# Hybrid decoder trunk on one core: keys' low parts packed once instead of twice, and one weight cast placed behind the value evictions

## Chip, core and metric

The kernel runs on one core of a Trainium2 chip. The metric is the device time of one execution in microseconds (us); lower is better. One matrix engine (PE), a vector engine (DVE), a scalar engine (ACT), a general engine (POOL) and a queue engine (SP) work side by side; SP and POOL issue the DMAs that matter here.

## What is computed

Two layers over 512 tokens of width 1024 in float32. Each layer normalises x, multiplies it by a joint input matrix that feeds three head groups (a short gated convolution, differential attention with rotary, a Conformer convolution of 31 taps), adds the joint output projection to x, and then adds a SwiGLU block. The attention is the part around the change:

```python
q = apply_rope(q.reshape(b, s, 2, N_DIFF_HEADS, DIFF_HEAD_DIM), cos, sin)
k = apply_rope(k.reshape(b, s, 2, N_DIFF_HEADS, DIFF_HEAD_DIM), cos, sin)
v = v.reshape(b, s, N_DIFF_HEADS, DIFF_V_DIM)
...
sc = jnp.einsum("bqmhd,bkmhd->bmhqk", qi, k) * scale
p = jax.nn.softmax(jnp.where(mask, sc, -jnp.inf), axis=-1)
a = p[:, 0] - lam * p[:, 1]
return jnp.einsum("bhqk,bkhe->bqhe", a, v)
```

There are four heads of two maps (m = 0, 1) with 64 channels each and 128-dim values.

## The kernel before

**Products in three passes.** Every float32 operand of a large product is split into a high part, rounded to the format fp32r in which PE multiplies, and a low part, the rest. A product is then three matmuls, high by high, high by low and low by high (`mm3`, lines 182 to 188).

**The weight pipeline.** All weights lie in one list of units of 512 KB in the order of use. `load` (line 110) brings a unit into one of three raw buffers, through POOL's queue for units 5 to 32 of a layer and through SP's for the rest. A unit is two halves, and each half is one tile `w` of [128, 2, 512] out of six. `prep` (line 124) fills it: ACT casts raw to the high part (line 135); then either DVE subtracts it from raw (lines 144 and 154), or, for most halves of the attention's stretch, ACT writes minus raw (line 137) and a DMA of POOL adds the weights to it from memory (line 138). That is, such a half costs ACT two instructions and POOL one DMA `w<-wu`. `next_half` (line 152) hands out the next half and calls `prep` for the ones ahead, up to five. While the list `held` is not empty, the furthest half is written down there instead of being prepared, and `release` (line 171) prepares what was written down later. Each engine executes in the order in which the program is written, so the place of `prep` in the code sets the place of its casts on ACT.

**Queries and keys.** `qk_units` computes the even and odd halves of the rotary pairs of two heads on PE, `turn_qk` (line 408) rotates them on DVE into tiles `ro`, and `split_and_pack` (line 425) splits them into `hl` (high and low) and moves the pieces to where the scores want them, with 16 DMAs of SP per call. For the queries, `pq` holds for each map the high part in partitions 0 to 63 and the low part in 64 to 127. For the keys, `pk` has four planes of [128, 512]: plane 2m holds the high part in both halves of the partitions, plane 2m+1 the low part in both halves. One DMA for each of the 16 pieces moves 32 partitions of 2 x 512 values (128 KB). There are two `pk` tiles (two heads of a pair) and two buffers, so that both pairs of both layers use the same two buffers. The scores (`Pair.scores`, lines 489 to 491) are, for each map, one matmul of `pq` with plane 2m, one with plane 2m+1, and one that adds the causal mask.

**Values.** `values` (line 453) multiplies h by the values' weights, with eight halves of weights and four PSUM results. ACT evicts the four results into `vt` (line 467). The results lie in both buffers of the PSUM pool `sc`, and the scores need a buffer of that pool: the first scores wait for the first two evictions.

**Slots.** After the values the program goes slot by slot (`slot`, line 774): PE does the scores of block b, six wide matmuls of filler work (`fill(2)`, two weight blocks), the attention values of block b-2, the transposes `pT` of block b-1, and six more wide matmuls. Between them DVE finds the maxima `nm` of the scores (line 493), does one tap of the 31-tap convolution (line 578) and combines the two maps into `e` (line 507), and ACT does the exponentials (line 497). The transposes of block b-1 wait for `e` of that block. During the values, `each` puts three taps behind each of the eight weight halves on DVE. The filler is the second pair's queries and keys first, then the short convolution.

Of the kernel before, what the change touches and what calls it, by code (L numbers as in the profile page):

```python
# [19 lines left out]
F32 = mybir.dt.float32  # L20
F32R = mybir.dt.float32r
# [7 lines left out]
S = 512  # L29
L = 2  # L30
P = 128
# [4 lines left out]
HD = 64  # L36
# [42 lines left out]
def trunk(ctx, tc, xT, pos, wu, cv, lamv, cst, out):  # L79
    nc = tc.nc  # L80
    V, A, G, T = nc.vector, nc.scalar, nc.gpsimd, nc.tensor

    def pool(name, bufs, **kw):
        return ctx.enter_context(tc.tile_pool(name=name, bufs=bufs, **kw))
    cp = pool("cp", 1)
# [4 lines left out]
    pk = pool("pk", 2)  # L90
# [32 lines left out]
    def prep(i, ahead=True):  # L123


        if i >= 2 * L * UNITS or i in wtiles:
            return
        u, half = divmod(i, 2)
        load(u)
        for k in range(1, 2 + half if ahead else 1):  # L130
            load(u + k)
        raw = wraw[u][:, half, :]
        t = pw.tile([P, 2, 4 * P], F32R, tag="w", name=f"w{i}")
        wtiles[i] = t
        A.copy(t[:, 0, :], raw)  # L135
        if 4 <= u % UNITS < 30 and (i % 3 == 1 or u % UNITS >= 12):
            A.mul(t[:, 1, :], raw, -1.0)  # L137
            G.dma_start(t[:, 1, :], wu[u, :, 4 * P * half:4 * P * half + 4 * P], accum_op=ALU.add)  # L138
        else:
            sub = functools.partial(V.tensor_sub, t[:, 1, :], raw, t[:, 0, :].bitcast(F32))  # L140
            if ordered[0] and i > 5:
                subs.append(sub)
            else:
                sub()  # L144
# [17 lines left out]
    held = []  # L162

    def release():

        for i in held[1:]:
            prep(i)
        del held[:]
# [21 lines left out]
    def side_by_side(n):  # L190


        for k in range(KC - n):
            w = next_half()
            for j in range(4):
                yield k, j, w
        ws = [next_half() for _ in range(n)]
        for j in range(4):
            for k in range(n):
                yield KC - n + k, j, ws[k]  # L200

    def four(name):
        ps = [sc.tile([P, 2, S], F32, tag="sc", name=f"{name}{i}") for i in range(2)]
        return [ps[i // 2][:, i % 2, :] for i in range(4)]
# [11 lines left out]
    def start():  # L216


        nc.sync.dma_start(cvt, cv)
        nc.sync.dma_start(x[0], xT[0])  # L220
        load(0)
        nc.sync.dma_start(x[1], xT[1])
        load(1)
        nc.sync.dma_start(x[2], xT[2])
        nc.sync.dma_start(x[3], xT[3])
        load(2)
        nc.sync.dma_start(x[4], xT[4])
        ones_d = cp.tile([P, P], F32, name="ones_d")
        pi = pt.tile([P, P], I32, tag="t", name="posi")
        G.dma_start(pi, pos)  # L230
        lv = pt.tile([P, L, 4, HD], F32, tag="t", name="lv")
        G.dma_start(lv, lamv.partition_broadcast(P))
        G.dma_start(ones_d, cst[:, 1, :])
        cs = pt.tile([P, 2, P], F32, tag="t", name="cs")
        G.dma_start(cs, cst[:, 0::2, :])
        warm = sm.tile([P, 1], F32, tag="nm", name="warm")
        V.memset(warm, 0.0)
        A.activation(warm, warm, AF.Sin)

        wz = pt.tile([P, S], mybir.dt.bfloat16, tag="t", name="wz")  # L240
        V.memset(wz, 0.0)
        wp = tp.tile([P, S], F32, tag="tp", name="wp")
        for _ in range(10):
            T.matmul(wp, lhsT=wz[:, :P], rhs=wz, start=True, stop=True)
        ones_r = cp.tile([P, P], F32R, name="ones_r")
        idr = cp.tile([P, P], F32R, name="idr")
        maskr = cp.tile([P, P], F32R, name="maskr")
        G.tensor_copy(ones_r, ones_d)
        G.tensor_copy(idr, cs[:, 0, :])
        G.tensor_copy(maskr, cs[:, 1, :])  # L250
        consts.update(ones_d=ones_d, ones_r=ones_r, idr=idr, maskr=maskr, ident=idr.bitcast(F32), pi=pi, lv=lv)
# [133 lines left out]
            yield  # L385

    pending = []
    gates = []

    def later():  # L390

        while pending:
            pending.pop(0)()
# [15 lines left out]
    def turn_qk(isk, ps, cosr, sinr, packs):  # L409

        t = [pt.tile([P, S], F32, tag="t", name=f"ro{i}") for i in range(4)]
        V.tensor_mul(t[0], ps[0], cosr)
        V.tensor_mul(t[1], ps[0], sinr)
        yield
        V.tensor_mul(t[2], ps[1], sinr)
        V.tensor_mul(t[3], ps[1], cosr)
        V.tensor_sub(t[0], t[0], t[2])
        V.tensor_add(t[1], t[1], t[3])
        if not packs:
            packs += [[pk.tile([P, n, S], F32R, tag=tag, name="p" + tag) for tag, n in (("q", 2), ("k", 4))]  # L420
                      for _ in range(2)]
        pending.append(functools.partial(split_and_pack, isk, t, packs))
        yield

    def split_and_pack(isk, t, packs):
        hls = [pr.tile([P, 2, S], F32R, tag="hl", name="hl") for _ in range(2)]
        for ab in range(2):
            if isk:
                A.copy(hls[ab][:, 0, :], t[ab])
            else:  # L430
                A.mul(hls[ab][:, 0, :], t[ab], QS)
        for ab in range(2):
            o, hl = t[ab], hls[ab]
            if isk:
                V.tensor_sub(hl[:, 1, :], o, hl[:, 0, :].bitcast(F32))
            else:
                V.scalar_tensor_tensor(hl[:, 1, :], o, QS, hl[:, 0, :].bitcast(F32), ALU.mult, ALU.subtract)
        for hh in range(2):
            q, k = packs[hh]
            for ab in range(2):  # L440
                hl = hls[ab]
                for m in range(2):
                    src = slice(64 * hh + 32 * m, 64 * hh + 32 * m + 32)
                    for d in range(2):
                        dst = slice(64 * d + 32 * ab, 64 * d + 32 * ab + 32)
                        eng = nc.sync
                        if isk:
                            eng.dma_start(k[dst, 2 * m:2 * m + 2, :].bitcast(F32), hl[src].bitcast(F32))
                        else:
                            eng.dma_start(q[dst, m, :].bitcast(F32), hl[src, d, :].bitcast(F32))  # L450

    def values(h, rT, each):
        ws = four("v")
        for n, (k, b, w) in enumerate(side_by_side(1)):
            t = slice(b * P, b * P + P)
            T.matmul(ws[b], lhsT=h[k][:, 0, t], rhs=w[:, 0, :], start=k == 0, stop=False)
            T.matmul(ws[b], lhsT=h[k][:, 0, t], rhs=w[:, 1, :], start=False, stop=False)
            T.matmul(ws[b], lhsT=h[k][:, 1, t], rhs=w[:, 0, :], start=False, stop=k == KC - 1)
            if n == 3:
                later()  # L460
            if n % 4 == 3:
                each(n // 4)
        vt = []
        for b in range(4):
            if b % 2 == 0:
                t = pv.tile([P, 2, S], F32, tag="v", name=f"vt{b}")
            A.activation(t[:, b % 2, :], ws[b], AF.Copy, scale=rT[:, b:b + 1])
            vt.append(t[:, b % 2, :])
        return vt

    class Pair:
# [170 lines left out]
    def mixing(l, h, run, each):  # L642
# [3 lines left out]
        packs = [[], []]  # L646


        pq = [acc.tile([P, S], F32, tag="acc", name="qk") for _ in range(2)] if l == 0 else []
# [8 lines left out]
        if l == 0:  # L658
            start()

            hs = []

            def chunk(k):
                h.append(make_h(k, C_MIXG))
                if k:
                    hs.append(add_square(k - 1, hs[-1] if hs else None, V, True))
            rt = rope_tables()
            next(rt)
            prep(0, False)
            chunk(0)  # L670
            prep(1, False)
            chunk(1)
            next(rt)
            lam = lambdas()
            for k in range(6):
                lead[0] = (1, 2, 2, 3, 3, 3)[k]
                chunks([k])
                if k < 3:
                    nc.sync.dma_start(x[k + 5], xT[k + 5])
                chunk(k + 2)  # L680
                if k == 0:
                    state["tab"] = next(rt)
                if k == 1:
                    next(lam)
            hs.append(add_square(KC - 1, hs[-1], V, True))
            run = hs[-1]
            lead[0] = AHEAD - 1
        else:
            chunks(range(6))
# [237 lines left out]
    for l in range(L):  # L927
# [24 lines left out]
        for half in range(2):  # L952
            acts = []
            for f in range(FH):
# [8 lines left out]
                t = pt.tile([P, S], F32, tag="t", name="tg")  # L963
# [128 lines left out]
```

## Time and profile before

| what | value |
| --- | --- |
| median of 3 runs | 1172.51 us (1172.22 to 1177.48) |
| the profiled execution's own time | 1169.26 us |
| its span in the profile | 1167.4 us |
| PE busy | 1137.1 us, 97% of the span |
| DVE, ACT, POOL busy | 637.2, 502.6, 198.5 us |
| mean granted TensorE clock | 0.986 of full |
| DMA traffic | 141.68 MB in 50342 packets |

The terms of the prediction are read from one execution, the profiled one; the runs without a profile lie 3.25 us higher in the median. PE has work for nearly the whole span, so time is won or lost where PE waits, or where it works at the lower of its two clock levels.

### The profile page before, as it was taken

Reading aid. Unit: us, or ns where it says so; the run is one execution under the profiler, and the core shown is the slowest. Engines: PE = TensorE matmul, PEld = TensorE weight load, DVE = VectorE, ACT = ScalarE, POOL = GpSimd, SP = SyncE. Lnnn points to the kernel's source line nnn. Section 1 sums busy time; section 2 is a strip of 40 time slices with the busy share of each in tenths; the row PEclk is TensorE's granted clock in tenths of the full one; section 3 lists DMA queues with packets and bytes.
Section 4 is the critical chain, followed back from the end, with each engine's and each line's share of the span. In section 5 each row is a group of like instructions: output and inputs, shape, how many; then the busy total and the mean of one; then the engine's idle time right before and its main releaser. Section 6 shows DMA issues by size and latency. Waiting matters only on the chain.

```text
span 1167.4 us, 14339 instructions
## 1 busy us (share of the span) xinstructions
PE 1137.1 (97%) x5238; PEld 943.8 (81%) x5238; DVE 637.2 (55%) x1140; ACT 502.6 (43%) x1034; POOL 198.5 (17%) x229
## 2 busy tenths in 40 slices
PE   8989899999999999999999899999999999999995
PEld 6878787788888888888888788877888888888885
DVE  6777786654443344444448788657444333444445
ACT  6546566643332233333334467765333222333323
POOL 2222223311100011010112222332111000011001
PEclk9989899999999999999999899999999999999998
DMA  7785847432332322322337878663223223223212
GB/s 228 190 211 130 197 109 165 106 126 91 104 95 90 109 91 94 105 90 99 102 98 177 195 170 190 139 158 97 102 90 106 93 91 108 91 94 105 90 55 73
DMA packets 50342, 141.68 MB, mean 121 GB/s; under 512 B 7104, under 2 KB 9408, under 8 KB 50272
## 3 DMA queue, kind: packets, MB, share of 16 engines
q1 hardware_dynamic: 29888, 88.79, 23.7%
q0 software_dynamic: 20384, 51.98, 19.5%
q8 instruction: 41, 0.67, 0.2%
q14 instruction: 29, 0.24, 0.1%
HBM read 125.93 MB, written 2.23 MB: 110 GB/s over the span
## 4 chain that ended last, share of the span: by engine, by line
PE 85%; DMA 4%; DVE 4%; issue 3%; ACT 2%; SPq 1%; POOL 1%; DVEq 0%; ACTq 0%; POOLq 0%
PE od L186 8%; PE od L188 8%; PE od L187 8%; PE gp L188 7%; PE gp L187 7%; PE up L187 7%; PE up L188 7%; PE up L186 7%; PE gp L186 6%; PE qk L186 3%; DMA raw<-wu 2%; PE qk L187 2%; PE qk L188 2%; PE cc L186 1%; PE cc L187 1%
## 5 line engine op out<-in xcount | busy, mean ns | idle before, releaser
L135 ACT CAST w<-raw 128x512 fp32r<-128x512 f32 x384 | 237.6, 622 | 495.1 <-PE od L188 146.0
L144 DVE TENSOR_TENSOR w<-raw,w 128x512 fp32r<-128x512 f32 x265 | 187.1, 707 | 239.8 <-ACT w L135 239.2
L966 POOL TENSOR_TENSOR tg<-tg,r 128x512 f32<-128x512 f32 x44 | 57.8, 1316 | 520.3 <-ACT tg L965 510.7
L187 PE MATMUL gp<-h,w 128*128 128x512 f32 x352 | 137.2, 390 | 0.6 <-DVE h L263 0.6
L186 PE MATMUL up<-h,w 128*128 128x512 f32 x352 | 137.2, 390 | 0.1
L188 PE MATMUL gp<-h,w 128*128 128x512 f32 x352 | 137.1, 390 | 0.0
L186 PE MATMUL gp<-h,w 128*128 128x512 f32 x352 | 137.1, 390 | 0.0
L187 PE MATMUL up<-h,w 128*128 128x512 f32 x352 | 137.0, 389 | 0.0
L188 PE MATMUL up<-h,w 128*128 128x512 f32 x352 | 137.0, 389 | 0.0
L186 PE MATMUL od<-act,w 128*128 128x512 f32 x328 | 127.6, 389 | 0.0
L187 PE MATMUL od<-act,w 128*128 128x512 f32 x328 | 127.6, 389 | 0.0
L188 PE MATMUL od<-act,w 128*128 128x512 f32 x328 | 127.6, 389 | 0.0
L138 POOL DMA_DIRECT2D w<-wu x82 | 72.7, 887 | 240.0 <-ACT w L137 217.9
L578 DVE SCALAR_TENSOR_TENSOR acc<-pad,cvt,acc 128x511 f32<-128x511 f32 (+14 forms) x120 | 88.0, 734 | 2.8
L187 PEld LDWEIGHTS gp<-h,w 128*128 128x128 f32 x352 | 66.1, 188 | 15.1 <-DVE h L263 1.5
L186 PEld LDWEIGHTS up<-h,w 128*128 128x128 f32 x352 | 66.1, 188 | 14.6 <-DVE x L932 1.0
L186 PEld LDWEIGHTS gp<-h,w 128*128 128x128 f32 x352 | 66.1, 188 | 14.1 <-ACT h L262 0.5
L188 PEld LDWEIGHTS up<-h,w 128*128 128x128 f32 x352 | 66.1, 188 | 13.8
L188 PEld LDWEIGHTS gp<-h,w 128*128 128x128 f32 x352 | 66.1, 188 | 13.6
L187 PEld LDWEIGHTS up<-h,w 128*128 128x128 f32 x352 | 66.1, 188 | 13.6
L188 PEld LDWEIGHTS od<-act,w 128*128 128x128 f32 x328 | 61.6, 188 | 12.9
L187 PEld LDWEIGHTS od<-act,w 128*128 128x128 f32 x328 | 61.6, 188 | 12.7
(255 smaller groups left out, 1982.0 us busy)
## 6 DMA issues: line engine op xcount, KB each, us to landing
raw<-wu SPq DMA_DIRECT2D x135, 512.0 KB, 3.5
raw<-wu POOLq DMA_DIRECT2D x56, 512.0 KB, 6.0
w<-wu POOLq DMA_DIRECT2D x82, 256.0 KB, 4.8
pk<-hl SPq DMA_DIRECT2D x64, 128.0 KB, 6.3
pq<-hl SPq DMA_DIRECT2D x64, 64.0 KB, 3.7
x<-xT SPq DMA_DIRECT2D x8, 256.0 KB, 7.5
yT<-fo SPq DMA_DIRECT2D x8, 256.0 KB, 2.5
raw<-wu SPq DMA_DIRECT2D x2, 256.0 KB, 4.9
```

Source lines behind the costliest of these rows:

```text
L135: A.copy(t[:, 0, :], raw)
L138: G.dma_start(t[:, 1, :], wu[u, :, 4 * P * half:4 * P * half + 4 * P], accum_op=ALU.add)
L144: sub()
L186: T.matmul(ps, lhsT=hi, rhs=rh[:, 0, :], start=first, stop=False)
L187: T.matmul(ps, lhsT=hi, rhs=rh[:, 1, :], start=False, stop=False)
L188: T.matmul(ps, lhsT=lo, rhs=rh[:, 0, :], start=False, stop=last)
L578: V.scalar_tensor_tensor(a[:, d:], pad[:, :S - d], cvt[:, c - d:c - d + 1], a[:, d:], ALU.mult, ALU.add)
L966: G.tensor_mul(t, t, r)
```

## The change

Three things. The keys' tiles become two permanent tiles `pk0` and `pk1`; the lower 64 partitions of planes 1 and 3 are set to zero once, by four memsets on POOL in layer 0. The DMAs of the keys leave these places out: of the 16 of a call, eight move 32 x 1024 values as before and eight move 32 x 512. So the second matmul of the scores multiplies the queries' high part with the keys' low part, and leaves out low by low, which stood in it before. Third, `values` puts a mark into `held` after the sixth of the eight halves, and calls `release` behind the evictions: the furthest halves that the last two halves of the values ask for are noted, and only what is still noted at the end is prepared behind the evictions.

```diff
+    keys = [cp.tile([P, 4, S], F32R, name=f"pk{hh}") for hh in range(2)]
+
+    def zero_rows():
+        for t in keys:
+            for m in range(2):
+                G.memset(t[HD:, 2 * m + 1, :].bitcast(F32), 0.0)
...
         if not packs:
-            packs += [[pk.tile([P, n, S], F32R, tag=tag, name="p" + tag) for tag, n in (("q", 2), ("k", 4))]
-                      for _ in range(2)]
+            packs += [[pk.tile([P, 2, S], F32R, tag="q", name="pq"), keys[hh]] for hh in range(2)]
...
-                        if isk:
+                        if isk and d == 0:
                             eng.dma_start(k[dst, 2 * m:2 * m + 2, :].bitcast(F32), hl[src].bitcast(F32))
+                        elif isk:
+                            eng.dma_start(k[dst, 2 * m, :].bitcast(F32), hl[src, 0, :].bitcast(F32))
...
             if n % 4 == 3:
                 each(n // 4)
+            if n == 23:
+                held.append(None)
         vt = []
         for b in range(4):
             if b % 2 == 0:
                 t = pv.tile([P, 2, S], F32, tag="v", name=f"vt{b}")
             A.activation(t[:, b % 2, :], ws[b], AF.Copy, scale=rT[:, b:b + 1])
             vt.append(t[:, b % 2, :])
+        release()
         return vt
...
             run = hs[-1]
+            zero_rows()
             lead[0] = AHEAD - 1
```

On ACT, around the evictions of layer 0 (w is a weight half, raw its unit, vt a value result), before:

```order
L135 CAST w_763<-raw_703 128x512
L137 ACTIVATE w_763<-raw_703 128x512
L135 CAST w_784<-raw_703 128x512
L137 ACTIVATE w_784<-raw_703 128x512
L135 CAST w_803<-raw_742 128x512
L137 ACTIVATE w_803<-raw_742 128x512
L467 ACTIVATE vt_822<-v_638,rT 128x512 x2
L467 ACTIVATE vt_825<-v_639,rT 128x512 x2
L497 ACTIVATE e,lsum<-ps,nm 128x128 x2
```

and with the change:

```order
L135 CAST w_767<-raw_707 128x512
L137 ACTIVATE w_767<-raw_707 128x512
L135 CAST w_803<-raw_707 128x512
L137 ACTIVATE w_803<-raw_707 128x512
L477 ACTIVATE vt_822<-v_642,rT 128x512 x2
L477 ACTIVATE vt_825<-v_643,rT 128x512 x2
L135 CAST w_828<-raw_746 128x512
L137 ACTIVATE w_828<-raw_746 128x512
L508 ACTIVATE e,lsum<-ps,nm 128x128 x2
```

One half's pair of instructions, the first of the unit raw_742 (raw_746 in the change), has moved behind the four evictions and stays ahead of the first exponentials; in layer 1 the same pair moves. The orders of PE and DVE are the same in both programs.

On POOL, at the place of the memsets in layer 0 (cosr is the cosine table, fetched from memory):

```order
L118 DMA raw_328<-wu 128x1024
L138 DMA w_345<-wu 128x512
L118 DMA raw_367<-wu 128x1024
L394 MEMSET pk_109 64x512 x2
L394 MEMSET pk_110 64x512 x2
L709 DMA cosr<-tab_dram 32x512 x4
L118 DMA raw_445<-wu 128x1024
```

The four memsets stand ahead of the four cosine DMAs and of the weight loads that follow; nothing else on POOL has moved.

## Rows read from the trace of the kernel before

**Rows 1.** Waits of PE over the span: us in total, times, longest.
```profile
PE ps L489 <- ACT vt L467: 7.3, 2, 4.2
PE ps L489 <- DMA pk<-hl: 5.6, 2, 4.4
...
PE ssps L301 <- DVE fo L897: 1.6, 1, 1.6
```

**Rows 2.** Timeline of ACT, layer 0: start us, us, instruction, [idle before <-releaser].
```profile
74.56 0.63 ACT L137 ACTIVATE w<-raw 128x512 fp32r<-128x512 f32 x1
77.73 0.62 ACT L135 CAST w<-raw 128x512 fp32r<-128x512 f32 x1 [2.54 <-DMA raw<-wu]
...
78.78 2.41 ACT L467 ACTIVATE vt<-v,rT 128x512 f32<-128x512 f32 x4
```

**Rows 3.** Timeline of PE, layer 0.
```profile
80.08 0.48 PE L489 MATMUL ps<-pk,pq 128*128 128x128 f32 x1 [4.21 <-ACT vt L467]
...
86.63 0.28 PE L489 MATMUL ps<-pk,pq 128*128 128x256 f32 x1
...
88.72 0.27 PE L516 MATMUL pT<-idr,e 128*128 128x128 f32 x1
```

**Rows 4.** Timeline of PE, layer 1.
```profile
653.62 0.47 PE L489 MATMUL ps<-pk,pq 128*128 128x128 f32 x1 [3.14 <-ACT vt L467]
...
662.19 0.27 PE L516 MATMUL pT<-idr,e 128*128 128x128 f32 x1
```

**Rows 5.** Stretches: busy us of each engine (count), PEclk, DMA share, GB/s.
```profile
79.80:86.50 6.70, 6.42 (x18) 5.35 (x19) 3.48 (x8) 3.23 (x9) 1.65 (x3) 0.50 0.93 232
134.40:141.10 6.70, 5.85 (x15) 4.66 (x16) 3.92 (x8) 2.46 (x7) 0.85 (x1) 0.50 1.01 241
...
653.20:659.90 6.70, 6.28 (x18) 5.22 (x19) 3.74 (x8) 3.37 (x9) 1.79 (x3) 0.50 1.05 265
...
1152.00:1156.00 4.00, 2.42 (x18) 1.94 (x17) 1.93 (x5) 1.90 (x5) 2.14 (x4) 1.00 0.03 11
```

**Rows 6.** Timeline of DVE, both layers.
```profile
69.97 11.53 DVE L578 SCALAR_TENSOR_TENSOR acc<-pad,cvt,acc 128x503 f32<-128x503 f32 x15
81.67 0.42 DVE L493 TENSOR_REDUCE nm<-ps 128x2 f32<-128x256 f32 x1 [0.17 <-PE ps L491]
...
83.47 0.35 DVE L507 SCALAR_TENSOR_TENSOR e<-e,c 128x128 f32<-128x128 f32 x1
...
643.72 11.45 DVE L578 SCALAR_TENSOR_TENSOR acc<-pad,cvt,acc 128x498 f32<-128x498 f32 x15
...
657.01 0.35 DVE L507 SCALAR_TENSOR_TENSOR e<-e,c 128x128 f32<-128x128 f32 x1
```

**Rows 7.** Chain that ended last: start us, us, what (a wide filler matmul; keys of pair 1).
```profile
107.80 0.23 PE qk L187
...
130.67 4.57 DMA pk<-hl
...
700.01 5.14 DMA pk<-hl
```

**Rows 8.** Timeline of ACT, layer 1.
```profile
648.32 0.62 ACT L137 ACTIVATE w<-raw 128x512 fp32r<-128x512 f32 x1
```

**Rows 9.** The stretch in which pair 1's keys are packed, columns as in rows 5.
```profile
126.00:131.00 5.00, 4.83 (x25) 3.90 (x23) 4.12 (x9) 4.24 (x12) 1.01 (x3) 1.00 1.03 227
```

**Rows 10.** POOL's two-input operation, of the page's costliest groups: busy us, mean ns.
```profile
L966 POOL TENSOR_TENSOR tg<-tg,r 128x512 f32<-128x512 f32 x44 | 57.8, 1316 | 520.3 <-ACT tg L965 510.7
```

**Rows 11.** DMA issues: out<-in, engine, op xcount, KB each, median us to landing.
```profile
pk<-hl SPq DMA_DIRECT2D x64, 128.0 KB, 6.3
...
cosr<-tab_dram POOLq DMA_DIRECT2D x8, 64.0 KB, 4.9
```

**Rows 12.** Timelines of POOL and of DVE around the cosine table, layer 0.
```profile
28.45 2.24 POOL L697 DMA_DIRECT2D cosr<-tab_dram  x4
...
40.81 0.69 DVE L703 TENSOR_TENSOR cosr<-cosr,r 128x512 f32<-128x512 f32 x1 [1.35 <-ACT r L340]
```

**Rows 13.** Landing of the DMA w<-wu that POOL issues at 67.1 us.
```profile
DMA to landing us min/median/max: 12.4/12.4/12.4
```

## Prediction

> **What bounds the kernel now.** The page first: PE is busy for 97% of the span, so only its waits and its clock can be won back. The list of PE's waits [rows 1] names two causes of weight: the first scores wait for the value evictions (7.3 us, once in each layer), and scores wait for the packed keys (5.6 us in two waits, 4.4 and 1.2). Then the timeline of ACT [rows 2] says why the evictions are late: the cast at 77.73 stands ahead of them, and ACT sat idle 2.54 us before it, for a weight transfer that had not landed. The evictions start only at 78.78, and PE, free since 80.08 - 4.21 = 75.87 [rows 3], starts the scores 1.30 us after that. In layer 1 PE waits 3.14 us at the same place [rows 4].
>
> The stretches [rows 5] show what each of these waits costs beside its own length: behind the value wait of layer 0, behind the long key wait and behind the value wait of layer 1 the granted clock is 0.50, the lower level of 1.2 GHz, for at least 6.7 us, in which full speed would have done the same work in half the time. Two waits of the profile are too short for that: the clock is 1.00 around the wait of 1.6 us near the end [rows 1, 5].
>
> Last the timeline of DVE [rows 6], because it is next in line: it does fifteen taps without a pause from 69.97 to 81.50 and reaches the first maxima `nm` at 81.67, having waited only 0.17 us for PE. The combined `e`, on which PE's first transposes hang, ends at 83.47 + 0.35 = 83.82. In layer 1 the taps end at 643.72 + 11.45 = 655.17 and `e` at 657.36.
>
> **The change, part by part.**
>
> *The cast behind the evictions, layer 0.* ACT's instruction ahead of the late cast starts at 74.56 [rows 2]; its neighbours follow one another 0.53 us apart, so ACT is free for the evictions at 75.09, not at 78.78. With the same 1.30 us to PE, the scores start at 76.39 instead of 80.08, a wait of 0.5 us, and no fall of the clock. That would save 3.7 us of wait and half of PE's 6.42 busy us at the low clock [rows 5], 6.9 us. But PE doesn't get that far. From the second scores to the first transposes it needs 88.72 - 86.63 = 2.09 us at full clock [rows 3]; of these 6 x 0.23 = 1.4 are six wide matmuls [rows 7], so that the first slot (scores and twelve wide ones) takes 3.5. PE stands before the transposes at 76.39 + 3.5 + 2.09 = 82.0, and `e` is there at 83.82 less DVE's 0.17 of waiting, 83.65, since DVE's taps are not moved. So PE waits a new 1.7 us, and with 0.1 for the handover passes the transposes at some 83.75 instead of 88.72: **4.97 us** won. Were the evictions earlier still, this would be the same.
>
> *Layer 1.* ACT is free at 648.32 + 0.53 = 648.85 [rows 8], before PE ends the values at 653.62 - 3.14 = 650.48 [rows 4], so nothing is left of the first wait. PE stands before the transposes at 650.5 + 3.5 + 2.09 = 656.1, `e` ends at 657.36, a new wait of 1.3 us; passed at 657.46 instead of 662.19: **4.73 us**.
>
> *What the moved cast delays.* Its transfer lands just before 77.73, when the four evictions (2.41 us from 75.09) are through at 77.5. So the cast stays where it was in time, and so does POOL's DMA behind it; the exponentials queued behind it on ACT wait for `nm` until after 81.9 anyway. Cost 0.
>
> *Fewer bytes of keys.* Of each 16 key DMAs eight shrink from 128 to 64 KB; their number on SP stays. For the first head of pair 1 (eight DMAs, four smaller) that is 4 x 64 KB = 0.26 MB. The DMA engines are full while they move (share 1.03, 227 GB/s [rows 9]), so the last of the eight lands 0.26 MB / 227 GB/s = 1.15 us earlier than 130.67 + 4.57 = 135.24 [rows 7]. I take 1.1. Below, nothing is gained if the landing is all latency. Above, 2.2 us, if the other queue's transfers that share the engines are held up in proportion and give back as much again. In layer 0 the key wait of 4.4 falls to 3.3 us: **1.1 us**, and the clock still falls, as it did behind the 3.14 us of layer 1 [rows 4, 5]. In layer 1 the keys land at 700.01 + 5.14 = 705.15, and 1.1 of the 1.2 us wait goes: **1.1 us**. The other pairs' keys are not waited for. By the page "DMA: Bandwidth & Descriptors" of the Trainium skill, section "Queues, rings and completion order", a DMA engine takes turns between queues by whole packets; smaller packets of one queue then give back their own time and not the other queue's, which would keep the sum as it is, while sharing by bytes would bring it to 1159.4. No row here shows the turns.
>
> *The memsets.* Four on POOL, each between nothing and POOL's two-input operation of that width, 1.32 us [rows 10]; at most 5.3 us together. I take the upper end. Behind them stand the cosine DMAs, issued by 28.45 + 2.24 = 30.69, landing 4.9 us later at the median [rows 11, 12], 35.6; DVE reads the table at 40.81, and waited there for ACT, not for it. That is 5.2 us of cover: cost 0. With that cover gone, a lateness of DVE at 40.81 would pass on to the queries.
>
> *Permanent key tiles.* Two buffers served all pairs before and two do now, so the key DMAs wait for the same scores. The second score matmul runs over 128 rows as before, zeros included. Cost 0.
>
> The sum is 4.97 + 4.73 + 1.1 + 1.1 = 11.9 us. The profiled execution's 1169.26 us would become 1157.4. The median of the runs is 3.25 us higher, 1172.51, and I make the forecast against it: **1160.6 us**, 1.0% less.
>
> **The rivals.**
>
> *The clock falls in the new wait.* My 1.7 us in layer 0 can be 2.2 if the evictions come earlier through a faster weight transfer (scores at 75.87). The trace has the clock kept around 1.6 us and lost behind 3.14; 2.2 is nearer to the first. If it falls, it costs the 3.2 us again: 1163.8. "TensorE: Matmul & The Clock Gate" of the Trainium skill, Part 1, says that the low clock is the default and that only activity keeps the high one, so this way is open wherever PE idles; the trace agrees at its three slow stretches.
>
> *The key wait in layer 0 gets short enough to keep the clock.* With 2.2 us won, 2.2 are left, again between the two bounds. Then 1.1 more in wait and some 2.9 us of slow clock (half of PE's 5.85 busy us there) go: 1156.6. For it: the DMA engines are full. Against it: it needs the upper bound.
>
> *DVE doesn't hold PE back.* If the taps ran ahead, the value waits would give 6.9 and 3.1 + 3.1 = 6.2 us in place of 4.97 and 4.73: 3.4 more, 1157.2. Against it: DVE has no pause in the fifteen taps.
>
> *The change doesn't do what it says.* One more cast stays ahead of the evictions and hangs on an earlier transfer. If that lands later by as much as the moved one waited, little is won: between 1167 and 1172.5. Against it: less traffic, not more, goes beside it.
>
> *Slower: the weights become the wait.* PE asks for the second filler half in the second slot, at 76.39 + 3.5 + 0.7 = 80.6 in place of 87.3. The DMA that completes it was issued at 67.1 and took 12.4 us [rows 13]: 79.5, so 1.1 us of room is left. It decides from 80.6 on. If it landed 2.75 us late in both layers, the wait and 3.2 for the clock would eat the 11.9; 6 us late in both gives 2 x 9.2 - 11.9 = 6.5 us slower, 1179. Against it: the keys' share of that traffic becomes smaller.
>
> **How the numbers follow.** Forecast 45%; clock lost in the new wait 25%; key wait short 10%; DVE no bound 5%; little done 11%; slower 4%. About 0.5% (5.9 us) is what a measurement of this kernel can tell from no change; the border is 1166.6. The first four are faster, less 2% for mishaps: 0.83. Little done, and those, lie within it: 0.13. The range goes from 1155.5 (key wait short, and 1 us of spread) to 1167 (clock lost in the new wait, and keys winning nothing): it leaves out most of the last two cases and little else.
>
> **What would show it.** PE's wait for `vt` falls from 7.3 to under 1.5 us. A new wait of PE's transposes for DVE's `e` appears, 1 to 2.3 us in each layer. The slow stretches near 80 and 653 are gone, the one near 135 (some 5 us earlier now) stays. DMA traffic falls by 32 x 64 KB, 2.1 MB. The key wait falls to about 3.3 us. I am wrong if the transposes don't wait, if PE waits for weights in the first slots, or if DVE's first `nm` isn't within 0.5 us of 81.5.

## Result, and the profile after

The changed kernel takes 1158.71 us in the median of 4 runs (1157.70 to 1159.33), beside 1173.11 us for the kernel before; the ratio is 0.9875, 95% interval [0.9842, 0.9907]. The profiled execution of the change has 1159.32 us of its own time, a span of 1157.5 us and a mean granted clock of 0.991; it moves 139.58 MB, 2.1 MB less than before. The profiled pair differs by 9.9 us, the medians by 14.4.

The waits of PE (us in total, times, longest), to be read beside [rows 1]:

```profile
PE ps L500 <- DMA pk<-hl: 3.8, 2, 3.5
PE pT L527 <- DVE e L518: 3.7, 2, 2.2
...
PE pT L527 <- DVE yb L565: 0.7, 1, 0.7
```

The 7.3 us for the value evictions are gone from the list. The transposes' wait for `e` has taken their place, and the keys' wait is 3.8 us in place of 5.6. Next the timeline of ACT in layer 0, as [rows 2]:

```profile
73.26 0.63 ACT L137 ACTIVATE w<-raw 128x512 fp32r<-128x512 f32 x1
74.60 2.62 ACT L477 ACTIVATE vt<-v,rT 128x512 f32<-128x512 f32 x4 [0.71 <-PE v L466]
77.11 0.62 ACT L135 CAST w<-raw 128x512 fp32r<-128x512 f32 x1
```

The cast stands behind the evictions, which now wait for PE and not for a weight transfer. The timeline of PE, as [rows 3, 4], with the key wait of layer 0 and two later places:

```profile
75.92 0.33 PE L500 MATMUL ps<-pk,pq 128*128 128x128 f32 x1
...
83.89 0.33 PE L527 MATMUL pT<-idr,e 128*128 128x128 f32 x1 [2.20 <-DVE e L518]
...
129.47 0.30 PE L500 MATMUL ps<-pk,pq 128*128 128x128 f32 x1 [3.52 <-DMA pk<-hl]
...
187.00 1.05 PE L301 MATMUL ssps<-ones_d,lnsq 128*128 128x1 f32 x8 [0.87 <-DVE yb L565]
...
652.29 0.33 PE L527 MATMUL pT<-idr,e 128*128 128x128 f32 x1 [1.54 <-DVE e L518]
...
701.23 0.33 PE L527 MATMUL pT<-idr,e 128*128 128x128 f32 x1 [0.72 <-DVE yb L565]
```

PE goes into the first scores without a wait and stands before the transposes. The timeline of DVE says why, as [rows 6]:

```profile
70.24 11.53 DVE L589 SCALAR_TENSOR_TENSOR acc<-pad,cvt,acc 128x503 f32<-128x503 f32 x15
81.68 0.42 DVE L504 TENSOR_REDUCE nm<-ps 128x2 f32<-128x256 f32 x1
...
83.48 0.35 DVE L518 SCALAR_TENSOR_TENSOR e<-e,c 128x128 f32<-128x128 f32 x1
...
638.72 11.45 DVE L589 SCALAR_TENSOR_TENSOR acc<-pad,cvt,acc 128x498 f32<-128x498 f32 x15
...
651.89 0.35 DVE L518 SCALAR_TENSOR_TENSOR e<-e,c 128x128 f32<-128x128 f32 x1
```

In layer 0 the fifteen taps start 0.27 us later than before, and `e` ends at 83.83 us where it ended at 83.82: DVE has gained nothing, PE has come up to it. The stretches, columns as in [rows 5]:

```profile
76.40:83.10 6.70, 5.29 (x28) 4.18 (x27) 6.22 (x10) 2.83 (x9) 1.42 (x2) 1.00 1.06 257
127.20:130.60 3.40, 1.13 (x7) 1.01 (x8) 1.25 (x3) 0.11 (x1) 1.03 (x2) 1.00 1.07 205
130.70:134.00 3.30, 3.30 (x10) 2.56 (x9) 2.89 (x7) 2.24 (x7) 0.77 (x1) 0.50 1.05 283
645.00:652.00 7.00, 5.75 (x30) 4.64 (x30) 6.47 (x12) 3.76 (x10) 1.42 (x2) 1.00 1.06 254
188.70:192.00 3.30, 3.30 (x9) 2.59 (x8) 2.25 (x13) 1.53 (x5) 0.00 (x0) 0.50 0.66 138
```

The granted clock is 1.00 in both value stages, where it was 0.50. Behind the key wait it is 0.50, the lower level of 1.2 GHz, but for about 3.4 us, not 6.7. A new slow stretch stands at 188.7, behind the eight one-column matmuls and the 0.87 us of wait at 187.00.

Both programs issue the same 5238 matmuls in the same order, so the two timelines of PE can be laid side by side, matmul by matmul. A gain is the growth of PE's lead over the kernel before at that place:

| place | predicted gain, us | measured, us |
| --- | --- | --- |
| value stage, layer 0 | 4.97 | 4.83 |
| keys, layer 0: the wait | 1.1 | 0.95 |
| keys, layer 0: the clock behind it | 0 | 1.17 |
| slow stretch at 188.7 | 0 | -1.58 |
| the rest up to layer 1 | 0 | 0.15 |
| value stage, layer 1 | 4.73 | 4.36 |
| keys, layer 1 | 1.1 | 0.84 |
| transposes at 701.23, wait for DVE's `yb` | 0 | -0.86 |
| sum | 11.9 | 9.86 |

Two questions are left: is DVE's row of taps what holds PE in the value stages, and why do the medians differ by 4.5 us more than the profiled pair?

### The profile page after: what moved, and what is told of

The parts are those of the page before. It is cut to its first block, busy times and chain, and to the rows that moved or that the text cites. A ratio compares the mean times of both kernels' runs of the same rounds, so it can differ in the third digit from the quotient of the medians.

```text
span 1157.5 us, 14341 instructions
## 1 busy us (share of the span) xinstructions
PE 1131.8 (98%) x5238; PEld 939.0 (81%) x5238; DVE 636.7 (55%) x1140; ACT 502.7 (43%) x1034; POOL 200.0 (17%) x233
## 2 busy tenths in 40 slices
DMA packets 50342, 139.58 MB, mean 121 GB/s; under 512 B 7104, under 2 KB 9408, under 8 KB 50272
## 4 chain that ended last, share of the span: by engine, by line
PE 81%; DVE 8%; DMA 4%; issue 3%; ACT 2%; SPq 1%; POOL 0%; DVEq 0%; ACTq 0%; POOLq 0%
PE od L186 8%; PE od L187 8%; PE od L188 8%; PE gp L188 7%; PE gp L187 7%; PE up L188 7%; PE up L187 7%; PE up L186 7%; PE gp L186 7%; DVE acc L589 3%; DMA pq<-hl 2%; PE qk L187 2%; PE qk L186 2%; PE qk L188 2%; DMA raw<-wu 1%
```

## Experiments

The runs were timed in four groups, each beside the kernel before on one chip: the kernel before again, the two parts and the first run of the moved taps (before: 1172.20 us in the median); the busy matmuls, the two queues, the change again and the three edits at once (1173.64); the moved taps again and with busy matmuls (1172.54); the two with a later load (1172.12).

### The kernel before again, and each part alone

The first run is the kernel before, unaltered.

> The kernel before, profiled once more. Its profiled execution took 1169.3 us, but its four runs without a profile took 1172.2 to 1177.5. Theory (the clock differs between executions): this profile shows the same waits of PE as the first (7.3 us for the value evictions, 5.6 us for the keys) to 0.5 us, and if its own time is 3 us or more above 1169.3, the slow-clock stretches are longer or one more in number by about twice that. Rival (the waits themselves vary): the slow stretches are the three of before, some 20 us with those at start and end, and a wait differs by 2 us or more. Time ratio to before 1.00 within 0.3%.

It took 1173.66 us (1168.00 to 1177.62 in 12 runs). Its profiled execution was a long one, 1177.62 us, 8.4 us above the first profile. PE's wait for the keys in layer 1 (its timeline), and the stretch behind it:

```profile
709.45 0.45 PE L489 MATMUL ps<-pk,pq 128*128 128x128 f32 x1 [3.93 <-DMA pk<-hl]
```

```profile
709.00:715.60 6.60, 6.16 (x17) 4.92 (x18) 3.92 (x8) 2.45 (x7) 0.85 (x1) 0.50 1.07 255
```

In the first profile this wait was 1.2 us [rows 1] and left the clock alone. Here it is 3.93 us and the clock falls. So a wait differs by more than 2 us, as the rival has it, and the clock adds as much again: the lag behind the first profile grows in this one place from 1.32 to 6.94 us, by 5.6. The execution that the sum was read from was one in which the keys of layer 1 came early; that is most of the difference between its 1169.26 us and this one.

The second run has the keys' part of the change alone: no mark in `held`, no release behind the evictions.

```
-            if n == 23:
-                held.append(None)
...
-        release()
         return vt
```

> The change with its first two parts alone: zero rows set once, shorter key transfers; no mark in the list held, no release behind the evictions. The cast stands ahead of the evictions again. Theory (the gain is the order on ACT, and the keys are about 1 us per wait): the weight transfer in front of that cast lands about 1.5 us earlier than before, as it did in the changed kernel (76.0 against 77.6), so the value waits of PE fall only to about 2.7 and 2 us from 4.2 and 3.1; the key waits fall to about 3.5 and 0.3. Time 4 to 6 us below before, 8 to 10 above the changed kernel, more if the clock holds. Rival (the lighter DMA traffic does it, the order on ACT matters little): the value waits are under 1 us and the time is within 2 us of the changed kernel.

It took 1162.40 us (1157.50 to 1163.74), ratio 0.9909 [0.9883, 0.9935]. The value waits are there about as expected (2.4 and 2.2 us). The time is a miss: it is 9.8 us below before in the medians, where 4 to 6 were expected and the prediction gave the keys 2.2. ACT, then PE, and the stretch behind:

```profile
76.04 0.62 ACT L135 CAST w<-raw 128x512 fp32r<-128x512 f32 x1 [2.72 <-PE v L466]
...
77.10 2.40 ACT L475 ACTIVATE vt<-v,rT 128x512 f32<-128x512 f32 x4
```

```profile
78.40 0.33 PE L497 MATMUL ps<-pk,pq 128*128 128x128 f32 x1 [2.44 <-ACT vt L475]
```

```profile
79.70:83.00 3.30, 3.30 (x9) 2.59 (x8) 2.99 (x6) 0.99 (x5) 0.00 (x0) 0.50 1.05 268
```

Before, this cast waited for its weight transfer and ran at 77.73 [rows 2]; here the transfer is no longer what comes last. The likely cause, argued and not tried by itself, is that the first pair's keys, which move beside it, have fewer bytes. How much of it is the keys' doing is open, since PE's wait before the first scores differs between executions of one order on ACT too: with keys and cast as before it was 4.21 and 3.14 us in the two layers of the first profile, 5.01 and 3.48 in the second, and 3.23 and 2.01 in the last run below. In these profiles the two parts shorten the same wait.

The third run has the mark and the release alone; the keys are packed as before.

```
             if n % 4 == 3:
                 each(n // 4)
+            if n == 23:
+                held.append(None)
...
+        release()
         return vt
```

> The change with its third part alone: the mark and the release behind the evictions; keys packed as before. Theory: the value waits are gone (0.5 us in layer 0 at most), the new waits of the transposes for DVE stand at 1.5 to 2.2 us in each layer, and the key waits stay at 4.4 and 1.2 us with the slow clock behind the long one. Time 9 to 11 us below before, 2 to 4 above the changed kernel. Rival (the order on ACT matters little): value waits of 2.5 us or more, time 3 us or less below before.

It took 1163.56 us (1162.53 to 1167.13), ratio 0.9932 [0.9909, 0.9956]. Of the value waits 1.01 us is left in layer 0, more than the 0.5 expected, and none in layer 1. Up to the transposes of layer 1 its PE is 10.30 us ahead of the first profile; then it loses 5.5 of these again, at the keys of layer 1, by its timeline of PE and the stretch behind:

```profile
697.89 0.45 PE L492 MATMUL ps<-pk,pq 128*128 128x128 f32 x1 [3.93 <-DMA pk<-hl]
```

```profile
697.20:703.80 6.60, 5.91 (x16) 4.68 (x17) 3.91 (x8) 2.45 (x7) 0.85 (x1) 0.50 1.05 246
```

The parts alone win 9.8 and 8.6 us in the medians, together 14.4: not additive, and by these profiles both work on the evictions.

### DVE's taps

Three taps per layer are moved out of the values' stage into later slots.

```
-        vt = values(h, rT, lambda n: tap(3))
+        vt = values(h, rT, lambda n: tap(3 if n < 5 else 2))
...
-            slot((pairs[0], b), 1)
+            slot((pairs[0], b), 2 if b in (3, 5, 7) else 1)
```

> The changed kernel with three of the 24 convolution taps of the values' stretch moved behind it: two instead of three taps for each of the last three weight halves, and two taps instead of one in the slots of blocks 3, 5 and 7. Theory (DVE's taps in front of the first maxima hold PE's transposes): three taps at 0.77 us bring the maxima forward by 2.3 us, the waits of the transposes for e (2.2 and 1.5 us) fall under 0.4 us each, and the time falls by 2.5 to 3.7 us, to about 1155.5. Rival 1 (the exponentials on ACT or the weights hold PE there): the waits stay or turn into waits for weights, and the time stays within 1 us. Rival 2 (the taps are dear where they go): the waits go, but PE waits as much in later slots, and the time stays.

It took 1153.73 us (1149.80 to 1156.56), ratio 0.9844 [0.9818, 0.9870]; run once more,

> The change with the three taps moved, once more beside the run above and on its chip: 5 us below the change, some 1153.7 us, if the first run was not a lucky one; the transposes pass at 82.9 in layer 0 and 647.2 in layer 1 within 0.5 us, and a key wait of some 2.8 us with a slow stretch of 3.4 us behind it stays.

it took 1157.13 us (1154.88 to 1158.35), ratio 0.9859 [0.9837, 0.9882], 3.4 us above the first run, where the same was expected. PE of the first of the two:

```profile
82.94 0.33 PE L527 MATMUL pT<-idr,e 128*128 128x128 f32 x1 [0.30 <-DVE e L518]
```

The transposes pass 0.95 us earlier than in the change (82.21 in the second run), and no wait of 1 us or more for `e` is left in either: the taps were what held PE. What the total gains is less sure, 2 to 5 us, since the key wait and the clock behind it differ between the two runs (a slow stretch of 3.4 us in one, 6.8 in the other).

### PE kept busy in the key wait

The change, with twelve matmuls whose result nobody reads ahead of pair 1's first scores in layer 0.

```
             if now:
+                if l == 0 and now[1] == 0 and now[0].g == 1:
+                    idle = av.tile([P, S], F32, tag="av", name="idle")
+                    for _ in range(12):
+                        T.matmul(idle, lhsT=consts["ones_r"], rhs=h[0][:, 0, :], start=True, stop=True)
                 now[0].scores(now[1])
```

> The change, with twelve extra wide matmuls (0.23 us each, 2.8 us in all; their result is read by nobody) ahead of the first scores of pair 1 in layer 0, where PE waited 3.52 us for the packed keys and a slow stretch of 3.4 us followed. Theory: the keys land when they land, and what the idle time costs beyond itself is the clock. The scores start as before (within 0.5 us of 129.5), PE's wait for pk there falls to about 0.7 us, the granted clock stays 1.00 behind it, and about 1.7 us is won (half of a slow stretch of 3.4 us; 3.4 us where the stretch would have been twice as long). Rival: the clock doesn't hang on this wait (the slow stretch stays at 130.6): no difference, or up to 2.8 us slower where the keys happen to land early.

It took 1156.24 us (1155.23 to 1156.71), beside 1159.29 for the change on the same chip (below). Its stretches, and PE:

```profile
125.80:128.60 2.80, 2.80 (x15) 2.34 (x14) 0.87 (x2) 1.66 (x4) 2.26 (x3) 1.00 1.07 290
128.70:132.00 3.30, 3.30 (x19) 2.85 (x18) 2.17 (x6) 2.06 (x7) 0.00 (x0) 1.00 1.08 223
```

```profile
125.81 3.00 PE L786 MATMUL idle<-h,ones_r 128*128 128x512 f32 x12
...
128.93 0.29 PE L500 MATMUL ps<-pk,pq 128*128 128x128 f32 x1
```

Work that nobody needs makes the kernel faster. The matmul that waited for the keys in the change (129.47) runs at 128.93, and the clock behind stays at the upper level of 2.4 GHz, worth 1.57 us to PE by 131.84; that is about the 1.7 expected. The rest of the 3 us isn't shown to come from the matmuls: beside the first profile of the change, this execution has no slow stretch at 188.7 (1.6 us), a wait for `e` of 0.62 us in layer 1 in place of 1.54, and keys that land earlier, and two executions of the change differ in the first of these too (below). Moved taps and busy matmuls together:

> The change with the three taps moved and the twelve extra matmuls in the key wait of layer 0, the keys all on SP. Theory (two separate causes: DVE's taps in the value stages, the clock behind the key wait): the gains add, 5 us and 2.4 us by the two single runs, so 7 us below the change, some 1151.5 us, with no wait for e, a clock of 1.00 behind the key wait, and no wait of the attention values for ACT as there was with keys issued by ACT. Rival (in the run with all three edits, which came out at 1155.97, the taps' gain was lost for another reason than ACT's issues): within 1.5 us of that run.

1152.29 us (1151.49 to 1155.59), ratio 0.9827 [0.9802, 0.9852]; the taps alone had 1157.13 beside it. The gains add, as far as the taps' own gain of 2 to 5 us lets one say.

### The change again, and its keys in two queues

> The change itself, unaltered: a second profile and more runs, for the spread of its waits. If the value stages are held by DVE's taps, PE passes the first transposes at 83.9 and 652.3 within 0.3 us again, with waits for e of about 2.2 and 1.5 us. If the keys' landing is what differs between executions, the waits for pk differ by 1 us or more from 3.5 and 0.3 us, and the span with them. If instead the span differs with the same waits, something else varies.

1159.29 us (1158.09 to 1160.60), ratio 0.9890 [0.9861, 0.9919]. The waits are the same: 2.35 and 1.48 us for `e`, 3.54 for the keys. The first transposes pass at 85.00, 1.1 us later than expected, of which 1.0 comes from the start of this execution, and at 651.65, as there is no slow stretch at 188.7. Where the change's waits repeat to 0.15 us in two profiles, those of the kernel before differ by 2.7.

```
-                        eng = nc.sync
+                        eng = nc.scalar if isk and d and not hh else nc.sync
```

> The change, with the four small key DMAs of each pair's first head issued by ACT in place of SP, so that the eight DMAs of that head stand in two queues and ACT pays for four issues per pair. Theory A (the DMA engines share out their time by queues, and the keys stand behind one another in one of two): with a share for a third queue the last key of pair 1 lands some 2 us earlier in both layers, PE's wait in layer 0 falls from 3.5 to about 1.5 us without a slow stretch behind it: 2 to 4 us faster. Theory B (the engines are full and the keys' own bytes set the landing): within 0.5 us of the change. Rival on the other side: ACT's issues hold up its evictions and casts: 1 to 3 us slower.

It took 1158.52 us (1157.13 to 1163.35), 0.8 us below the change and within its spread, though PE's wait for the keys in layer 0 is gone. ACT pays for the issues (its timeline), PE waits for ACT, and a weight load of POOL goes out later:

```profile
115.36 2.45 ACTq L456 DMA_DIRECT2D pk<-hl  x4
```

```profile
118.92 1.16 PE L542 MATMUL o<-vt,at 128*128 128x128 f32 x8 [1.70 <-ACT at L529]
```

```profile
122.58 0.88 POOL L118 DMA_DIRECT2D raw<-wu  x1
```

That the second queue ended the wait is therefore not shown. In the change this load goes out at 120.90, 0.44 us ahead of the eighth key DMA; here it goes out 4.4 us behind it, and the section on the transfers says what that is worth. In layer 1 the load is 5.6 us behind, and the eighth key still takes 6.5 us.

With the moved taps and the busy matmuls on top:

> The change with three edits at once: three taps moved out of the values' stage (5 us faster in its own run), the twelve extra matmuls in the key wait, and the four small key DMAs of each first head issued by ACT. If the three work on different waits, their gains add: 5 us from the taps, about 1.7 from the clock behind the key wait, and what the two queues give, less what the last two share (the same wait): 1150 to 1153 us. If moving the taps only makes PE arrive earlier at the keys' landing, the key wait grows by as much as it won in layer 0, and the sum stays within 1 us of the taps alone.

1155.97 us (1154.56 to 1162.16), ratio 0.9878 [0.9849, 0.9908]: the sum failed, and the same two edits without ACT's issues came to 1152.29.

### Which transfer goes first

What decides when a key lands? PE's scores wait for the eighth key DMA of pair 1. On POOL, a weight load of 512 KB is issued about when SP issues it. The profiles of before, of the change and of its parts, in order of how the two issues stand:

| program, layer | load issued, us after the eighth key | key: issue to landing, us | PE's wait, us |
| --- | --- | --- | --- |
| before, 0 | -1.26 | 8.1 | 4.4 |
| release alone, 0 | -1.19 | 8.2 | 4.6 |
| before again, 0 | -1.14 | 8.5 | 4.9 |
| keys alone, 0 | -0.54 | 6.7 | 2.5 |
| change, 0 | -0.44 | 7.9 | 3.5 |
| before again, 1 | 0.28 | 7.7 | 3.9 |
| release alone, 1 | 0.37 | 7.8 | 3.9 |
| before, 1 | 0.42 | 5.1 | 1.2 |
| change, 1 | 0.59 | 4.4 | 0.3 |
| keys alone, 1 | 0.68 | 4.1 | none |

Where the load goes out first, the key takes 6.7 to 8.5 us, and so it does with the old packing where the load is up to 0.37 us behind. Where it goes out later, the key takes 4 to 5. The second profile of the change (7.9 us with the load 0.44 us ahead, 4.5 with it 0.73 behind) and those of the moved taps and the busy matmuls fit in, but for the border: with the smaller keys a load 0.25 us behind was late enough, and the key took 4.2 us. The two runs with ACT's issues have the load 4.4 us or more behind, and their keys, in two queues, took 4.9 to 6.5 us. Two runs move the load, and on POOL what stands behind it, by memsets into the buffer that the load then fills. In the change with the moved taps, layer 0 only:

```
             eng = G if 4 < u % UNITS < 33 else nc.sync
+            if u == 21:
+                for _ in range(4):
+                    G.memset(wraw[u][:64, 0, :], 0.0)
```

> The change with the three taps moved, and four memsets (0.48 us each by the change's own trace, 1.9 us) on POOL ahead of one weight load of layer 0, the 512 KB one that POOL issued 0.46 and 0.71 us ahead of the eighth key DMA of pair 1 in the two profiles of the moved taps; so it now goes out about 1.2 us behind that DMA. In the profiles so far the eighth key DMA on SP took 6.7 to 8.5 us to land where that load went out ahead of it, and 4.1 to 5.1 us where it went out 0.42 us or more behind it. Theory (the last key queues behind the 512 KB in the DMA engines): it lands 4 to 5 us after its issue, PE's wait for pk in layer 0 falls from 2.8 to 3.5 us to under 0.8, no slow stretch follows, 3 to 6 us faster than the two runs of the moved taps (1153.7 and 1157.1): 1150 to 1152. Theory of bytes alone (landing set by how much the engines carry): it lands 7 us after its issue as before, no gain. Rival on the other side: the weights of that load come 1.9 us late and PE waits for them: a new wait for w of 1 to 2 us behind the key wait.

It took **1149.93 us** (1149.92 to 1150.72), ratio 0.9807 [0.9788, 0.9826], the fastest version here, and outside the change's interval; beside the moved taps alone, it is outside the interval of their second run and touches that of the first. Its POOL, SP and PE, and the stretch behind the keys:

```profile
119.57 2.25 POOL L120 MEMSET raw<- 64x512 f32 x4
122.12 0.55 POOL L121 DMA_DIRECT2D raw<-wu  x1 [0.30 <-POOL raw L120]
```

```profile
119.83 0.60 SPq L459 DMA_DIRECT2D pk<-hl  x1
```

```profile
124.43 0.30 PE L503 MATMUL ps<-pk,pq 128*128 128x128 f32 x1 [0.17 <-issue]
```

```profile
124.40:131.00 6.60, 5.84 (x31) 4.73 (x31) 5.15 (x10) 4.03 (x10) 2.80 (x4) 1.00 1.06 254
```

The key lands 4.4 us after its issue, PE waits 0.17 us, and the clock stays. PE is 6.3 us ahead of the second run with the moved taps when that run is at 134 us, 3.35 of it wait and 2.95 clock; 1.1 of it goes again at the next transposes, which wait 0.87 us for DVE's `yb`. No wait for `w` has come in behind it. In layer 1, where nothing is put ahead of it, the load goes out 0.43 us behind the eighth key, the key takes 5.3 us, and PE waits:

```profile
686.86 0.30 PE L503 MATMUL ps<-pk,pq 128*128 128x128 f32 x1 [1.38 <-DMA pk<-hl]
```

And the kernel before, with keys and casts as they were, five memsets ahead of the same load in both layers (`u % UNITS == 21`):

> The kernel before, keys packed as there, with five memsets (2.4 us) ahead of the same weight load in both layers, so that it goes out 1.1 us or more behind the eighth key DMA of pair 1 (in its profiles 1.26 and 1.14 us ahead of it in layer 0, 0.42 and 0.28 us behind it in layer 1). Theory of the queue: the eighth key lands some 5 us after its issue in both layers; the wait of 4.4 to 5.0 us in layer 0 falls to about 1.5 us and keeps the clock, the one in layer 1 is about 1 us in each execution: 6 us faster than before where layer 1's load had gone out late enough, 12 us where it had not; so a median near 1163 and a narrower spread than 1164.7 to 1178.4. Theory of bytes: both landings stay near 8 us, the median stays at 1172 to 1174. Rival: the gain is lost to later weights: waits of PE for w appear.

It took 1164.23 us (1160.79 to 1166.27), ratio 0.9931 [0.9913, 0.9950]. PE, and the landing of the eighth key in layer 1:

```profile
129.58 0.30 PE L492 MATMUL ps<-pk,pq 128*128 128x128 f32 x1 [1.32 <-DMA pk<-hl]
...
695.68 0.30 PE L492 MATMUL ps<-pk,pq 128*128 128x128 f32 x1 [1.05 <-DMA pk<-hl]
```

```profile
L451 SPq DMA_DIRECT2D pk<-hl x1: 675/675/675, 690.2 to 690.2; - x1
...
DMA to landing us min/median/max: 5.2/5.2/5.2
```

It moves as many bytes as before and wins 7.9 us in the medians by when a load is issued. The theory of bytes alone falls. The spread of its six runs, 5.5 us, is no narrower than that of before beside it (5.6), so that part of the expectation isn't borne out. Its profile is that of the fastest run. Of the 8.5 us by which it leads the first profile of before, 5.0 come at the keys of layer 0, and 2.4 and 2.5 in the value stages, each of which lies ahead of its layer's memsets; 1.4 go again elsewhere. PE at the values of layer 1, and the stretch behind:

```profile
645.43 0.33 PE L492 MATMUL ps<-pk,pq 128*128 128x128 f32 x1 [2.01 <-ACT vt L470]
```

```profile
647.00:650.30 3.30, 3.30 (x10) 2.56 (x9) 2.17 (x6) 1.84 (x6) 0.37 (x1) 0.50 1.10 246
```

## Why the prediction held, and where its steps were off

The forecast of 1160.6 us is 1.9 above the median, well inside the range.

**The value stages** were right by their mechanism. PE should be capped by DVE's taps, with new waits of 1.7 and 1.3 us; they are 2.20 and 1.54, and the transposes pass at 83.89 where 83.75 was predicted. The longer wait is the case named under the first rival, scores at about 75.87: they start at 75.92. The clock did not fall in it, nor in the second profile at 2.35 us, nor in that of the busy matmuls at 2.26, so that rival did not come true. It was close: in other runs value waits of 2.01, 2.22 and 2.44 us, ahead of the scores, were each followed by 3.4 us at the lower clock. By the Trainium skill ("TensorE: Matmul & The Clock Gate", Part 1) the low clock is the default and activity releases it. The stretches behind these waits agree, and the waits of 2.20 to 2.35 us that kept the clock show that the length of a wait alone doesn't decide. The rival in which DVE is no bound fell with the same rows, and the moved taps showed it from the other side. In layer 1 the gain is 4.36 instead of 4.73: PE's lead at that point was 5.5 us, but DVE's taps start only 5.0 us earlier (638.72 instead of 643.72) and `e` ends 5.1 earlier (652.24 instead of 657.36), so the cap came forward by less than PE did.

**The keys** were right in size, but not by the step given. That step is "the last of the eight lands 0.26 MB / 227 GB/s = 1.15 us earlier", with the landing taken from the chain's row of 130.67 + 4.57 [rows 7]. In layer 0 that row isn't the last of the eight: a key DMA issued at 130.67 is the twelfth of the 16, of the other head. The eighth is issued at 126.95 and takes 8.06 us, to 135.01; the landing is off by 0.23 us only, but the long flight of the eighth key stayed hidden. In layer 1 the chain's row is the eighth key. These are the rows of the twelfth key of layer 0, of the eighth for the kernel before (layers 0 and 1), then for the change:

```profile
L448 SPq DMA_DIRECT2D pk<-hl x1: 606/606/606, 130.7 to 130.7; - x1
...
DMA to landing us min/median/max: 6.7/6.7/6.7
```

```profile
L448 SPq DMA_DIRECT2D pk<-hl x1: 1720/1720/1720, 126.9 to 126.9; - x1
...
DMA to landing us min/median/max: 8.1/8.1/8.1
...
DMA to landing us min/median/max: 5.1/5.1/5.1
```

```profile
L456 SPq DMA_DIRECT2D pk<-hl x1: 597/597/597, 121.3 to 121.3; - x1
...
DMA to landing us min/median/max: 7.9/7.9/7.9
...
DMA to landing us min/median/max: 4.4/4.4/4.4
```

In layer 0 the eighth key's time from issue to landing fell by 0.17 us only. The other 0.84 of the 1.01 us comes from SP, which issues from the first to the eighth key in 4.94 us instead of 5.78; in layer 0 of the other profiles with all keys on SP it takes 5.55 to 5.70 us for the old keys and 4.8 to 5.2 for the smaller ones. Why SP issues faster wasn't tried. In layer 0 the load still goes out first; in layer 1 the key is now ahead of it by 0.59 us (0.73 in the second profile) in place of 0.42 (0.28).

**The sum against the medians.** By the profiled pair the change wins 9.9 us, less than the 11.9 predicted: the slow stretch at 188.7 and the wait at 701.23, both behind DVE's `yb` and unforeseen, gave back 2.4 in all, and the shorter slow stretch behind the keys brought 1.17. By the medians it wins 14.4, more than predicted. The missing term is the clock and wait at the keys of layer 1, which the first profile had escaped: 5.6 us in the second one. Setting a sum read from one execution against a median was fair only if the 3.25 us between them stay, and by the second profile a part of them was this race, which the change mostly ends. So it is in part luck that the forecast came within 1.9 us: the sum gave 2.0 us too much for the profiled pair, and left out 4.5 us of the medians. That the race is won in each run of the change is not shown; it is in both of its profiles.

**The small steps.** No cost of the memsets shows: they take 1.93 us for four, and the cosine DMAs behind them are issued by 31.3, long before DVE reads the table. The moved cast starts at 77.11, and no wait of PE for it shows. PE's waits for weights in the first slots, the rival on the slower side, did not come. The permanent key tiles cost nothing that shows.

What stays open: why the key lands so late behind the load. By the page "DMA: Bandwidth & Descriptors" of the Trainium skill (section "Queues, rings and completion order") a DMA engine takes turns between queues packet by packet. It would follow that 64 or 128 KB in one queue need not wait for 512 KB in another. The traces show a key that lands within 1.2 us of the load that went out ahead of it, in each of the five upper rows of the table. The measurement decides here; which of the engines or rings holds the key wasn't tried.

## What to carry to other kernels

When a small transfer is waited for, look at what large one is issued within a microsecond of it on another queue, and settle their order in the program; that was worth 3 us of wait and 3 of clock at one place here, 1 of it given back to the next wait, for a delay of about 3 us of a load that had time. Before a sum is read from one profile, profile the unchanged kernel twice: a wait that differs between the two may be a race, and a change that ends it wins more than its own step says. A wait has two prices, its length and the clock behind it; where the wait can't go, work that nobody needs can still save the second.

## What the runs showed of the hardware that was not expected

- The eighth key DMA, with all keys in one queue, took 6.7 to 8.5 us from issue to landing behind a 512 KB load of another queue, and 4.1 to 5.3 us where it went out ahead of the load by 0.42 us or more.
- The same wait of PE may lose the clock in one execution and not in another. The eight one-column matmuls with 0.87 us of wait before them kept the clock in the kernel before (at 193.95), were followed by a slow stretch at 188.7 in the first profile of the change, and by none there in the second, which has one at the same place of layer 1 (752.9 to 756.1, clock 0.50). Behind like key waits of 2.8 and 3.5 us the slow stretches of the moved taps were 3.4 and 6.8 us long. A wait of 2.01 us before the scores of layer 1 lost the clock for 3.4 us, and one of 2.35 us before the transposes of layer 0 did not.
- Four issues of DMAs took ACT's queue 2.45 us, during which its other work stood still.
- A memset of 64 x 512 values took POOL 0.48 us at the start of layer 0, and 0.56 to 0.64 us while the keys were packed.
